# Attention scores of a two-layer encoder trunk: two stacked full-height products, or three half-height products per head

## The chip, the cores and the metric

The kernel runs on one core of one Trainium2 chip. The metric is the device time of one execution in microseconds; where several runs are given, their median. The profile is one execution recorded by the hardware profiler: TensorE's products and weight loads are listed apart (PE, PEld), VectorE is DVE, ScalarE is ACT, GpSimd is POOL, and SP is the queue that issues most transfers.

## What is computed

Two layers of an encoder trunk on 512 tokens of width 1024, in float32. In each layer a wide projection feeds three mixers in parallel, differential attention (4 heads, each with two query-key sets of 64 channels), a convolution module, and neighbourhood attention (8 heads of 64 channels on an 8 x 64 grid); gates merge them, and a gated feed-forward block and a gated input embedding follow. The parts that the change touches are the scores of the two attentions:

```python
# differential attention, per head: two score matrices from 64 channels each
s = jnp.einsum('bhcqd,bhckd->bhcqk', qi, k).astype(f32) * scale
a = jax.nn.softmax(s, axis=-1)
a = (a[:, :, 0] - lam * a[:, :, 1]).astype(v.dtype)
...
# neighbourhood attention, per head: 8 x 16 keys around each query, with a bias
s = jnp.einsum('bhwd,bhrwcd->bhwrc', q_r, kn).astype(jnp.float32) * scale
s = s + bias.transpose(0, 2, 1, 3)[None].astype(jnp.float32)
a = jax.nn.softmax(s.reshape(B, HC, GRID_W, KR * NA_KC), axis=-1)
```

## The kernel before

Everything is held transposed: channels on the 128 partitions, the 512 tokens along the free axis. A token's number in the kernel is its column times 8 plus its row, so that a neighbourhood is a window of keys: each of the four tiles of 128 queries sees 256 keys, which start at 0, 64, 192 and 256 (`KEY0`). TensorE multiplies in a reduced format (fp32r). To keep float32 accuracy every operand is split into a high part (rounded, on ScalarE) and a low part (the remainder, on VectorE); a product of two split operands takes three products, high x high, high x low and low x high (`mm3`, lines 177 to 179).

`layer` writes the order of TensorE's instructions by hand. Projections, gates and branches stream through `gemm`, and after every fourth chunk of three products a tick (12 products) passes. The attentions' units are generators which `later` puts into a queue; a unit starts a given number of ticks after its projection, with a gap to the next, and each `yield n` in it lets n ticks pass before it goes on. So the units' small products are dealt out between the projections' products of 512 columns. On the other engines a scheduler sets the order.

A pair of neighbourhood heads (`natten_in`) or one differential head (`diff_in`) has its queries and keys in one projection: 64 channels of one set (u = 0) on partitions 0 to 63 and of the other (u = 1) on 64 to 127. Before, the parts are written to tiles of their own ("kh" and "t", or "kh" and "rp"), and `stack` (line 660 issues the copies on SP's queue) builds stacked operands from them: for each set a query tile with the high part on 64 partitions and the low part on the other 64, a key tile in the same order, and a second key tile (`k2`, tag "x") in the opposite order. Then `scores` (line 811) needs two products over all 128 partitions for a set: the first gives high x high + low x low, the second high x low + low x high.

A neighbourhood unit (`natten_unit`) handles one head and one half of the queries, that is two query tiles: it loads one bias tile (line 702), makes the two score tiles, adds the bias and takes the maximum on VectorE (line 710), takes exponentials with their sums on ScalarE, then reciprocals (line 722) and scalings; two ticks later it transposes the probabilities on TensorE (lines 734 to 738), splits them, and two ticks later multiplies them with the values (lines 753, 754). A pair of heads has four units, a tick apart. A differential unit (`diff_unit`) handles one query tile of one head; `probs` makes its two score tiles of 512 keys, whose maxima VectorE takes (line 902). Score tiles lie in PSUM under the tag "sc", of which there are two, a bank each. SBUF tiles with a tag share as many buffers as the table `bufs` gives: qk 2, x 4, e 4, b 2, kh 2.

## Time and profile before

| | us |
|---|---|
| median of three runs (lowest, highest) | 1776.03 (1776.01, 1777.37) |
| span of the profiled execution | 1776.7 |
| HBM rate over the span | 125 GB/s |

The profiled execution's time is known as its span, from its first to its last instruction. A row of the page or of a view of the trace names the line, the engine, the operation, the tile written and the tiles read, the shape, the number of instructions, and their durations. Products overlap: a record goes on past the start of the next one, and the ends are modelled, so a product's cost in a stream is the distance between two starts. The rows themselves stand in the prediction, beside the sentences that use them.

### The profile page before, as it was taken

The numbers are of one execution on the slowest core, as the hardware profiler recorded it, in microseconds if no ns is written. First come the engines' busy times: TensorE is split into PE (matmuls) and PEld (weight loads), VectorE is DVE, ScalarE is ACT, GpSimd is POOL, SyncE is SP. The second block draws the span as 40 slices with busy tenths as digits, with TensorE's granted clock in tenths as the row PEclk, the third lists the DMA queues.
The fourth block names the chain that finished last, engine by engine and source line by source line (L and its number), as shares of the span: only waits on it lengthen the run. The fifth ranks groups of instructions, "written<-read, shape, count | busy, mean of one in ns | idle before, by whom it ended". The sixth has DMA issues, their size and how long they took to land.

```text
span 1776.7 us, 27451 instructions
## 1 busy us (share of the span) xinstructions
PE 1767.5 (99%) x10210; PEld 1559.6 (88%) x10210; DVE 1421.7 (80%) x2418; ACT 894.4 (50%) x1561; POOL 103.0 (6%) x146
## 2 busy tenths in 40 slices
PE   9999999999999999999999999999999999999998
PEld 7888888888899899998888888888888998989987
DVE  7878887998798587787776788889887976867776
ACT  5577555225565254454545765452356643534454
POOL 0000000000111010100000000000001110101000
PEclk9999999999999999999999999999999999999999
DMA  5666641334757366543447655423357664655332
GB/s 202 188 186 176 161 125 42 113 98 140 230 150 193 109 167 160 132 131 123 145 124 198 176 165 149 113 71 95 93 179 198 171 179 115 173 144 151 98 108 92
DMA packets 113509, 256.07 MB, mean 144 GB/s; under 512 B 14560, under 2 KB 19424, under 8 KB 113376
## 3 DMA queue, kind: packets, MB, share of 16 engines
q1 hardware_dynamic: 99984, 229.93, 42.3%
q0 software_dynamic: 12672, 23.07, 8.3%
q8 instruction: 81, 1.33, 0.3%
q10 hardware_dynamic: 720, 1.31, 0.2%
q14 instruction: 52, 0.43, 0.1%
HBM read 215.46 MB, written 7.34 MB: 125 GB/s over the span
## 4 chain that ended last, share of the span: by engine, by line
PE 96%; DVE 2%; ACT 1%; issue 0%; DMA 0%; POOL 0%; ACTq 0%; POOLq 0%; DVEq 0%
PE ffn_mm L1017 4%; PE ffn_mm L1019 4%; PE ffn_mm L177 4%; PE ffn_mm L179 4%; PE ffn_mm L178 4%; PE ffn_mm L1018 4%; PE ffn_sc L1019 3%; PE ffn_sc L1017 3%; PE ffn_sc L1018 3%; PE mergea_mm L177 2%; PE mergea_mm L178 2%; PE mergea_mm L179 2%; PE diff_sc L811 2%; PE gatec_mm L177 2%; PE gatec_mm L178 2%; PE gatec_mm L179 2%
## 5 line engine op out<-in xcount | busy, mean ns | idle before, releaser
L160 DVE SCALAR_TENSOR_TENSOR conv_z<-glu_z,pre_par,conv_z 128x512 f32<-128x512 f32 x240 | 179.4, 748 | 3.3
L143 ACT ACTIVATE ffn_wh<-ffn_wr 128x1024 fp32r<-128x1024 f32 (+1 forms) x92 | 92.7, 1014 | 111.7 <-PE ffn_mm L178 77.1
L987 POOL DMA_DIRECT2D ffn_qk<-w_fu x88 | 78.0, 990 | 605.7 <-DMA ffn_qk<-w_fu 414.7
L157 DVE TENSOR_TENSOR ffn_wl<-ffn_wr,ffn_wh 128x1024 fp32r<-128x1024 f32 (+1 forms) x92 | 107.4, 1173 | 5.4 <-ACT ffn_wh L143 4.9
L157 DVE TENSOR_TENSOR ffn_t<-ffn_mm,wo_rb 128x512 f32<-128x512 f32 (+1 forms) x64 | 38.6, 604 | 67.9 <-PE ffn_mm L179 67.8
L143 ACT ACTIVATE mergea_wh<-mergea_wr 128x1024 fp32r<-128x1024 f32 (+1 forms) x32 | 27.1, 846 | 96.8 <-PE mergea_mm L178 79.6
L143 ACT ACTIVATE ffn_wh<-ffn_qk 128x1024 fp32r<-128x1024 f32 x44 | 46.7, 1060 | 35.9 <-PE ffn_mm L178 15.7
L157 DVE TENSOR_TENSOR ffn_wl<-ffn_qk,ffn_wh 128x1024 fp32r<-128x1024 f32 x44 | 53.8, 1224 | 11.3 <-ACT ffn_wh L143 11.3
L157 DVE TENSOR_TENSOR ffn_t<-ffn_t,ffn_t 128x512 f32<-128x512 f32 (+1 forms) x46 | 31.3, 680 | 31.4 <-ACT ffn_t L143 30.9
L143 ACT ACTIVATE diff_a<-diff_sc,diff_s 128x512 f32<-128x512 f32 x32 | 22.0, 686 | 61.0 <-DVE diff_s L902 61.0
L177 PE MATMUL ffn_mm<-ffn_v,ffn_wh 128*128 128x512 f32 x132 | 51.4, 389 | 0.0
L178 PE MATMUL ffn_mm<-ffn_v,ffn_wh 128*128 128x512 f32 x132 | 51.4, 389 | 0.0
L179 PE MATMUL ffn_mm<-ffn_v,ffn_wl 128*128 128x512 f32 x132 | 51.3, 389 | 0.0
L177 PE MATMUL ffn_mm<-ffn_y,ffn_wh 128*128 128x512 f32 x132 | 51.3, 389 | 0.0
L178 PE MATMUL ffn_mm<-ffn_y,ffn_wh 128*128 128x512 f32 x132 | 51.3, 389 | 0.0
L179 PE MATMUL ffn_mm<-ffn_y,ffn_wl 128*128 128x512 f32 x132 | 51.3, 389 | 0.0
L1019 PE MATMUL ffn_mm<-wo_h,ffn_wl 128*128 128x256 f32 x176 | 49.8, 283 | 0.0
L1019 PE MATMUL ffn_sc<-wo_h,ffn_wl 128*128 128x256 f32 x176 | 49.8, 283 | 0.0
L1018 PE MATMUL ffn_mm<-wo_h,ffn_wh 128*128 128x256 f32 x176 | 49.8, 283 | 0.0
L1018 PE MATMUL ffn_sc<-wo_h,ffn_wh 128*128 128x256 f32 x176 | 49.8, 283 | 0.0
L1017 PE MATMUL ffn_sc<-wo_h,ffn_wh 128*128 128x256 f32 x176 | 49.8, 283 | 0.0
L1017 PE MATMUL ffn_mm<-wo_h,ffn_wh 128*128 128x256 f32 x176 | 49.8, 283 | 0.0
(876 smaller groups left out, 6588.6 us busy)
## 6 DMA issues: line engine op xcount, KB each, us to landing
ffn_qk<-w_fu POOLq DMA_DIRECT2D x88, 256.0 KB, 5.7
ffn_wr<-w_fg SPq DMA_DIRECT2D x44, 512.0 KB, 3.7
ffn_wr<-w_fd SPq DMA_DIRECT2D x32, 448.0 KB, 3.9
ffn_r<-w_fu SPq DMA_DIRECT2D x44, 256.0 KB, 3.7
ffn_qk<-w_fg SPq DMA_DIRECT2D x44, 256.0 KB, 4.3
ffn_qk<-w_fu SPq DMA_DIRECT2D x44, 256.0 KB, 4.6
natten_wr<-w_in SPq DMA_DIRECT2D x16, 512.0 KB, 4.3
natten_b<-bias SPq DMA_DIRECT2D x32, 256.0 KB, 4.0
```

The lines of the kernel that those rows point to most:

```text
L143: i = self.nc.scalar.activation(out, in_, func, **kw)
L157: return self.nc.vector.tensor_tensor(out, a, b, op)
L160: return self.nc.vector.scalar_tensor_tensor(out, a, s, b, op0, op1)
L177: mm(out, wh, ah, start=first, stop=False)
L178: mm(out, wh, al, start=False, stop=False)
L179: mm(out, wl, ah, start=False, stop=last)
L811: self.nc.tensor.matmul(out, st4[:, u, qs], st[:, ks], start=n == 0, stop=n == 1)
L987: nc.gpsimd.dma_start(q, wu[:, lo], accum_op=ALU.add)
L1017: mm(out, wh[:, c], bh, start=first and k == 0, stop=False, skip_group_check=True)
L1018: mm(out, wh[:, c], bl, start=False, stop=False, skip_group_check=True)
L1019: mm(out, wl[:, c], bh, start=False, stop=k == 3, skip_group_check=True)
```

## The change

- `natten_in` and `diff_in` write the high and the low parts straight into the query-key tile `st4`: index 0 and 1 are the queries' high and low parts, 2 and 3 the keys'. `stack` goes, with its copies and with `k2`. (`scores` stays in the file, but nothing calls it.)
- `both_scores` makes the scores of two sets at once: three products for each set (high x high, high x low, low x high), each over the 64 partitions on which its set lies, and in turn one of the lower half, one of the upper half. The two sets write to two score tiles.
- A neighbourhood unit handles both heads of a pair and one half of the queries: both heads' scores of the first query tile, a tick later those of the second; then reciprocals and scalings of both; two ticks later the first head's transposes and values (`natten_values`), and a tick later the second head's. There are two units for a pair, with a gap of two ticks.
- The bias lies sorted by pair and query tile, so that one transfer brings both heads. The probabilities of the second half of the queries lie in tiles of the tag "x" instead of "e".
- `probs` takes both score tiles first, makes their products together, and then goes on as before.

```diff
@@ -633,32 +633,21 @@
 
         self.phase = "natten"
         st4 = self.sb("qk", [P, 4, 512], F32R)
-        k2 = self.sb("x", [P, 2, 512], F32R)
         for s, off in enumerate((OFF_QC, OFF_KC)):
             ps = self.proj(off + pr * P)
             f = 1.0 if s else 0.125
-            nat, low = self.sb("kh", [P, 512], F32R), self.sb("t", [P, 512], F32R)
+            nat, low = st4[:, 2 * s], st4[:, 2 * s + 1]
             if pr == 0:
 
-                t = low.bitcast(F32)
+                t = self.sb("t", [P, 512])
                 self.stt(t, ps, f, self.rb, ALU.mult, ALU.mult)
                 ps, f = t, 1.0
             self.act(nat, ps, AF.Copy, scale=f)
             self.background(self.stt(low, ps, f, nat.bitcast(F32), ALU.mult, ALU.subtract),
                             self.bg["natten"])
-            self.stack(nat, low, st4[:, 2 * s:2 * s + 2], k2 if s else None)
         ys.append(self.sb("y", [P, 2, 512], F32R))
-        for n in range(4):
-            self.later(self.natten_unit(pr, n // 2, n % 2, st4, k2, st, ys[pr]), 6 if pr == 3 else 5 if pr else 10, 1)
-
-    def stack(self, nat, low, one, two):
-
-        for n, part in enumerate((nat, low)):
-            for st, r in ((one, 64 * n), (two, 64 - 64 * n)):
-                for u in range(2):
-                    if st is not None:
-                        self.nc.sync.dma_start(st[r:r + 64, u].bitcast(F32),
-                                               part[64 * u:64 * u + 64].bitcast(F32))
+        for half in range(2):
+            self.later(self.natten_unit(pr, half, st4, st, ys[pr]), 6 if pr == 3 else 5 if pr else 10, 2)
 
     def natten_v(self, st):
 
@@ -692,37 +681,49 @@
                     self.nc.sync.dma_start(vd[o:o + 64, n].bitcast(F32), edge.bitcast(F32))
             st["v", g] = vs[g], vd
 
-    def natten_unit(self, pr, half, u, st4, k2, st, y):
+    def natten_unit(self, pr, half, st4, st, y):
 
         nc, i = self.nc, self.i
-        mm = nc.tensor.matmul
-        head = 2 * pr + u
-        b = self.sb("b", [P, 2, NW])
-        with self.tc.high_priority(offset=100):
-            nc.sync.dma_start(b, self.a["bias"][i, head, half])
-        es = []
-        m = self.sb("s", [P, 6])
+        es, ms = ([], []), [self.sb("s", [P, 6]) for _ in range(2)]
         for t in range(2):
             qt = 2 * half + t
-            sc = self.ps("sc", (P, NW))
-            self.scores(sc, st4, k2, u, slice(qt * P, (qt + 1) * P),
-                        slice(KEY0[qt], KEY0[qt] + NW))
-            nc.vector.tensor_tensor_reduce(
-                out=b[:, t], in0=sc, in1=b[:, t], scale=-1.0, scalar=3.0e38,
-                op0=ALU.add, op1=ALU.min, accum_out=m[:, t:t + 1])
+            b = self.sb("b", [P, 2, NW])
+            with self.tc.high_priority(offset=100):
+                nc.sync.dma_start(b, self.a["bias"][i, pr, qt])
+            scs = [self.ps("sc", (P, NW)) for _ in range(2)]
+            self.both_scores(scs, st4, slice(qt * P, (qt + 1) * P),
+                             slice(KEY0[qt], KEY0[qt] + NW))
             wide = half != t
-            e = self.sb("e", [P, NW + 64 * wide])
-            own = slice(64 * (qt == 1), 64 * (qt == 1) + NW)
-            if wide:
-                pad = slice(0, 64) if qt == 1 else slice(NW, NW + 64)
-                nc.gpsimd.memset(e[:, pad], 0.0)
-            self.act(e[:, own], b[:, t], AF.Exp, table="exp", scale=-1.0, bias=m[:, t:t + 1],
-                     accum_out=m[:, 2 + t:3 + t])
-            es.append((e, e[:, own]))
-        nc.vector.reciprocal(m[:, 4:6], m[:, 2:4])
-        for t, (_, own) in enumerate(es):
-            self.act(own, own, AF.Copy, scale=m[:, 4 + t:5 + t])
+            if half:
+                both = self.sb("x", [P, 2, 512])
+            for u, (sc, m) in enumerate(zip(scs, ms)):
+                nc.vector.tensor_tensor_reduce(
+                    out=b[:, u], in0=sc, in1=b[:, u], scale=-1.0, scalar=3.0e38,
+                    op0=ALU.add, op1=ALU.min, accum_out=m[:, t:t + 1])
+                e = (both[:, u] if half else self.sb("e", [P, 512]))[:, :NW + 64 * wide]
+                own = slice(64 * (qt == 1), 64 * (qt == 1) + NW)
+                if wide:
+                    pad = slice(0, 64) if qt == 1 else slice(NW, NW + 64)
+                    nc.gpsimd.memset(e[:, pad], 0.0)
+                self.act(e[:, own], b[:, u], AF.Exp, table="exp", scale=-1.0, bias=m[:, t:t + 1],
+                         accum_out=m[:, 2 + t:3 + t])
+                es[u].append((e, e[:, own]))
+            if t == 0:
+                yield 1
+        for u, m in enumerate(ms):
+            nc.vector.reciprocal(m[:, 4:6], m[:, 2:4])
+            for t, (_, own) in enumerate(es[u]):
+                self.act(own, own, AF.Copy, scale=m[:, 4 + t:5 + t])
         yield 2
+        for u in range(2):
+            self.run(self.natten_values(pr, half, u, es[u], st, y))
+            if u == 0:
+                yield 1
+
+    def natten_values(self, pr, half, u, es, st, y):
+
+        nc = self.nc
+        mm = nc.tensor.matmul
         pt = self.ps("tr", (P, 2, 256))
         pt2 = self.ps("tr", (P, P))
         p2 = self.sb("a", [P, P], F32R)
@@ -810,6 +811,13 @@
         for n, st in enumerate((st4[:, 2 + u], k2[:, u])):
             self.nc.tensor.matmul(out, st4[:, u, qs], st[:, ks], start=n == 0, stop=n == 1)
 
+    def both_scores(self, outs, st4, qs, ks):
+
+        for n, (a, b) in enumerate(((0, 2), (0, 3), (1, 2))):
+            for u, out in enumerate(outs):
+                r = slice(64 * u, 64 * u + 64)
+                self.nc.tensor.matmul(out, st4[r, a, qs], st4[r, b, ks], start=n == 0, stop=n == 2)
+
     def diff_in(self, head, st, ys):
         self.phase = "diff"
         if head == 0:
@@ -819,7 +827,6 @@
                 self.nc.sync.dma_start(c, self.a["rope"][t])
                 st["tabs"].append(c)
         st4 = self.sb("qk", [P, 4, 512], F32R)
-        k2 = self.sb("x", [P, 2, 512], F32R)
         for s, off in enumerate((OFF_QA, OFF_KA)):
             ps = self.proj(off + head * P)
             raw, rot = self.sb("rp", [P, 512]), self.sb("rp", [P, 512])
@@ -830,22 +837,20 @@
             self.background(self.tt(raw, raw, st["tabs"][0], ALU.mult), self.bg["diff"])
             self.tt(rot, rot, st["tabs"][1], ALU.mult)
             self.tt(raw, raw, rot, ALU.add)
-            nat, low = self.sb("kh", [P, 512], F32R), raw.bitcast(F32R)
-            self.split(nat, low, raw)
-            self.stack(nat, low, st4[:, 2 * s:2 * s + 2], k2 if s else None)
+            self.split(st4[:, 2 * s], st4[:, 2 * s + 1], raw)
         box = dict(s0=self.sb("sm", [P, 4]))
         for qt in range(4):
-            self.later(self.diff_unit(head, qt, st4, k2, st, box, ys), 6 if head else 7, 2)
+            self.later(self.diff_unit(head, qt, st4, st, box, ys), 6 if head else 7, 2)
 
     def diff_v(self, g, st):
         self.phase = "diff"
         st["v", g] = self.values(self.a["w_va"][self.i, g], lambda v, a: ((v[:, 0:256], v[:, 256:512], a),))
 
-    def diff_unit(self, head, qt, st4, k2, st, box, ys):
+    def diff_unit(self, head, qt, st4, st, box, ys):
 
         nc, i = self.nc, self.i
         half, t = qt // 2, qt % 2
-        box[qt] = self.probs(st4, k2, qt, box["s0"])
+        box[qt] = self.probs(st4, qt, box["s0"])
         if t == 0:
             return
         yield 3
@@ -889,16 +894,16 @@
 
         yield from self.norm(sq, P, (1, 2), done, spread=False, eps=eps)
 
-    def probs(self, st4, k2, qt, s0):
+    def probs(self, st4, qt, s0):
 
 
         nc, i = self.nc, self.i
         qs = slice(qt * P, (qt + 1) * P)
         m = self.sb("s", [P, 10])
         es = []
-        for u in range(2):
-            sc = self.ps("sc")
-            self.scores(sc, st4, k2, u, qs, slice(0, 512))
+        scs = [self.ps("sc") for _ in range(2)]
+        self.both_scores(scs, st4, qs, slice(0, 512))
+        for u, sc in enumerate(scs):
             nc.vector.tensor_reduce(out=m[:, u:u + 1], in_=sc, op=ALU.max, axis=AX.X, negate=True)
             e = self.sb("e" if u else "a", [P, 512])
             self.act(e, sc, AF.Exp, table="exp", bias=m[:, u:u + 1],
@@ -1403,7 +1408,7 @@
         ok = (w[k][None, :] >= cs[q][:, None]) & (w[k][None, :] < cs[q][:, None] + NA_KC)
         out[:, :, qt] = np.where(ok, rpb[:, :, np.where(ok, ro, 0), np.where(ok, co, 0)],
                                  out[:, :, qt])
-    out = out.reshape(L, HC, 2, 2, P, NW).transpose(0, 1, 2, 4, 3, 5)
+    out = out.reshape(L, HC // 2, 2, 4, P, NW).transpose(0, 1, 3, 4, 2, 5)
     return np.ascontiguousarray(out)
 
 
```

## The prediction

> **What bounds the kernel now.** I read the head of the page first, then the waits of TensorE, then the two attention stages of layer 0.
>
> ```profile
> span 1776.7 us, 27451 instructions
> ...
> PE 1767.5 (99%) x10210; PEld 1559.6 (88%) x10210; DVE 1421.7 (80%) x2418; ACT 894.4 (50%) x1561; POOL 103.0 (6%) x146
> ...
> PEclk9999999999999999999999999999999999999999
> ...
> PE 96%; DVE 2%; ACT 1%; issue 0%; DMA 0%; POOL 0%; ACTq 0%; POOLq 0%; DVEq 0%
> ```
>
> TensorE is busy 1767.5 of 1776.7 us, at full clock, and the chain that ended last is 96% TensorE. A busy share of 99% alone could hide modelled ends, so the waits of that engine come next:
>
> ```profile
> PE pre_av L325 <- DVE pre_zeror L398: 1.1, 1, 1.1
> PE natten_tr L734 <- ACT natten_e L143: 0.3, 2, 0.2
> PE natten_tr L736 <- ACT natten_e L143: 0.3, 2, 0.2
> PE natten_tr L736 <- DVE natten_a L157: 0.2, 1, 0.2
> ```
>
> It waits 1.9 us in all, 1.1 of them at the start. The only waits of the attentions are 0.8 us, where the neighbourhood probabilities arrive late at their transposes. By stretches (both attentions' inputs and units; then the rest of differential attention and its neighbours):
>
> ```profile
> 70.00:172.00 102.00, 101.61 (x594) 88.73 (x593) 78.47 (x192) 74.20 (x179) 2.12 (x14) 1.00 0.69 188
> 172.00:320.00 148.00, 148.00 (x798) 127.07 (x798) 125.73 (x219) 76.93 (x154) 4.53 (x4) 1.00 0.41 113
> ```
>
> TensorE (the second number) fills both, ScalarE 74 of 102 us and VectorE 126 of 148. So the question is how much time the new score products take on TensorE and nothing else, unless another engine is made late.
>
> **The score products: what goes.** The line of scores has four rows of products, 128 of each width (64 of each row):
>
> ```profile
> L811 PE MATMUL natten_sc<-natten_qk x64: 277/283/366, 77.7 to 1043.5; 128*128 128x256 f32 x64
> L811 PE MATMUL natten_sc<-natten_x,natten_qk x64: 274/281/283, 77.8 to 1043.6; 128*128 128x256 f32 x64
> L811 PEld LDWEIGHTS diff_sc<-diff_qk x64: 187/188/192, 172.3 to 1167.3; 128*128 128x128 f32 x64
> L811 PE MATMUL diff_sc<-diff_qk x64: 389/396/478, 172.3 to 1167.5; 128*128 128x512 f32 x64
> L811 PE MATMUL diff_sc<-diff_x,diff_qk x64: 387/394/398, 172.6 to 1167.8; 128*128 128x512 f32 x64
> ```
>
> Their durations overlap, so a product's price is the distance to the next start, from the order of time:
>
> ```profile
> 77.68 0.28 PE L811 MATMUL natten_sc<-natten_qk 128*128 128x256 f32 x1
> 77.80 0.28 PE L811 MATMUL natten_sc<-natten_x,natten_qk 128*128 128x256 f32 x1
> 77.91 0.28 PE L811 MATMUL natten_sc<-natten_qk 128*128 128x256 f32 x1
> 78.03 0.28 PE L811 MATMUL natten_sc<-natten_x,natten_qk 128*128 128x256 f32 x1
> 78.15 0.40 PE L177 MATMUL natten_mm<-glu_h,natten_wh 128*128 128x512 f32 x1
> ...
> 172.63 0.39 PE L811 MATMUL diff_sc<-diff_x,diff_qk 128*128 128x512 f32 x1
> 172.86 0.39 PE L811 MATMUL diff_sc<-diff_qk 128*128 128x512 f32 x1
> 173.09 0.40 PE L811 MATMUL diff_sc<-diff_x,diff_qk 128*128 128x512 f32 x1
> 173.33 0.39 PE L177 MATMUL diff_mm<-glu_h,diff_wh 128*128 128x512 f32 x1
> ```
>
> Four neighbourhood products take 78.15 - 77.68 = 0.47 us, 0.117 each. A differential one takes (173.33 - 172.63) / 3 = 0.233, so four take 0.93. Each layer and attention has 16 such groups of four (four pairs of heads or four heads, four query tiles), so 32 groups of each: 32 x 0.47 = 15.0 us and 32 x 0.93 = 29.8 us, 44.8 us together.
>
> **What comes.** The same group becomes three pairs of products over 64 partitions, the two halves in turn. Before has no product of fewer than 128 rows, so a pair is bounded from both sides. If its two products run at the same time it costs one full product: 3 x 0.117 x 32 = 11.2 us and 3 x 0.233 x 32 = 22.4 us, 33.6 together, a gain of 11.2 us. If they run one after the other, six products per group cost twice that, 67.2 us, a loss of 22.4. I take the first: the two products read different partitions, hold different weights and write different banks (two tiles of "sc"), so neither needs what the other makes, and the list of waits shows no resource of TensorE at which products queue.
>
> The Trainium skill's page "TensorE: Matmul & The Clock Gate", "Part 3: Packing small matmuls — row/col tiling", says that products on different row groups run concurrently and gives 3.07x for four of them; no run here shows it. By it the pair would stand at the gain of 11.2 us.
>
> **The change of height.** Before and after each group are full-height products, so the array goes from full to half height and back: 2 x 64 = 128 times. The trace has no such change; the nearest one of kind is between transposes and products:
>
> ```profile
> 84.12 0.60 PE L736 MATMUL natten_tr<-pre_ident,natten_e 128*128 128x128 f32 x4
> 84.56 0.27 PE L738 MATMUL natten_tr<-pre_ident,natten_e 128*128 128x128 f32 x1
> 84.59 0.36 PE L811 MATMUL natten_sc<-natten_qk 128*128 128x256 f32 x1
> 84.79 0.28 PE L811 MATMUL natten_sc<-natten_x,natten_qk 128*128 128x256 f32 x1
> ```
>
> From the fifth transpose to the second score product are 0.23 us: a transpose, (84.56 - 84.12) / 4 = 0.11, and a score product, 0.12. That change costs nothing, and 0 is the lower end (a gain is excluded: nothing becomes shorter by a change). The upper end is that the array empties and the next weights are loaded only then: the tail of a record past the next start, 0.39 - 0.23 = 0.16 us, and one weight load, 0.19, so 0.35. I take the tail alone, 0.16: a transpose uses the array at the same height, so its 0 is the weaker neighbour, while weights are seen to load beside running products (loads busy 1559.6 us under 1767.5 us of products). 128 x 0.16 = 20.5 us (0 to 44.8).
>
> The page "TensorEngine Tiling (Array Packing)" of the Trainium skill, "Key Properties", speaks against the change: going over to another tiling mode, not just to another tile, drains the engine. It gives no price and no run here shows it; with the tail as the price the sum by that rule is the sum below, without it 1764.8 us.
>
> **The rest, costed at nothing.** The 192 copies that stacked queries and keys leave SP's queue (eight rows, 32 four times and 16 four times; the first and the last):
>
> ```profile
> L660 SPq DMA_DIRECT2D natten_qk<-natten_kh x32: 461/467/1325, 53.2 to 1011.7; - x32
> ...
> L660 SPq DMA_DIRECT2D diff_x<-diff_rp x16: 594/596/610, 163.3 to 1128.6; - x16
> ```
>
> No wait of TensorE names a DMA, and the units' starts are fixed by counted products, so the time that this frees (192 x about 0.55 us of issuing) goes into idle. The bias tiles stay 32 transfers of 256 KB, sorted by pair and query tile. The splits now write into the query-key tile itself, so ScalarE can wait for the scores of the head two before; those scores stand ahead of, or within 30 products (7 us) of, the end of the projection that the split follows, and in differential attention the rotation comes between. Behind such a wait stand the weight splits that TensorE needs, but the projections already run ahead; 0, at most 1 us for each of two heads a layer, 4 us.
>
> A neighbourhood unit of two heads goes as follows:
>
> ```profile
> L710 DVE CUSTOM_DVE_ANT_0 natten_b<-natten_sc,natten_b x64: 404/424/426, 78.1 to 1049.2; 128x256 f32<-128x256 f32 x64
> L143 ACT ACTIVATE natten_e<-natten_b,natten_s x64: 492/509/513, 79.1 to 1049.8; 128x256 f32<-128x256 f32 x64
> L143 ACT ACTIVATE natten_e<-natten_e,natten_s x64: 491/496/524, 80.7 to 1051.1; 128x256 f32<-128x256 f32 x64
> ```
>
> Before: two reductions, two exponentials, a reciprocal, two scalings, then transposes two ticks (24 products) later. After, the second half of a unit has the same two reductions and two exponentials, the first head's two scalings, and its transposes again two ticks later; the second head's scalings come behind and its transposes a tick later. The chain to the transposes keeps its length; 0, and where it is tight already (the four waits of 0.2 us) up to the two extra scalings, 4 x 1.0 = 4 us.
>
> **The sum.** 0 - 11.2 + 20.5 = +9.3 us. The profile's span of 1776.7 becomes 1786.0; it lies 0.7 above the median of 1776.0, inside the runs' 1776.0 to 1777.4, and I forecast 1786, not separating the two.
>
> **Rivals.** One, faster: the array changes its height for little. The place is the first product after each of the 128 changes; the price that decides is 11.2 / 128 = 0.088 us. At 0 it is 1764.8, at 0.06 (half a narrow product) 1772.5. For it: the transposes' 0, and weight loads that run beside products. Against: the narrow groups last only 0.35 us, so nothing in a group hides a price at both its ends.
>
> Two, much slower, the change not doing what it says: pairs don't overlap, because loads and products are issued in one line and each waits for the one before. 1776.0 + 22.4 = 1798.4 with free changes, 1818.9 with the tail, 1843 with the upper end. For it: no record of before has two products streaming at once, starts being 0.117 or 0.233 apart throughout. Against: all those products use all rows.
>
> Three, no change: the price lies at 0.06 to 0.115 us and eats the gain, 1772.5 to 1779.5.
>
> **How the numbers follow.** The forecast, overlap with a price of 0.115 to 0.35, has 0.37 and its own range 1779.5 to 1810; rival one 0.33; rival two 0.23; rival three 0.07. A difference under 0.2% (3.6 us) can't be told from none, which makes faster 0.33, within 0.07, slower 0.60. The range 1766 to 1812 leaves out the cheapest changes and the upper half of rival two, some 0.15.
>
> **What would show it.** In the order of time inside a group of six, starts in pairs with 0.23 us (wide) or 0.12 us (narrow) from pair to pair show the overlap; six starts that far apart show rival two. The distance from the sixth product to the projection behind it, and into the first, over 0.23 or 0.12, is the price of a change; if it is under 0.088 I am wrong about the sign. The line of scores should then take 54 us of TensorE's time where it took 44.8. If the groups agree and the time doesn't, the waits of TensorE on ScalarE (transposes of the neighbourhood) and on VectorE (score tiles not free) must have grown past the 1.9 us, and the terms put at nothing are where I went wrong.

## The result, and the profile after

The changed kernel takes 1799.95 us, the median of four runs (1799.67 to 1800.23); the kernel before takes 1776.70 beside it (1776.01 to 1778.10). The ratio is 1.0131 (95% interval 1.0116 to 1.0145): slower by 23.2 us where the forecast said 9.3. The profiled spans differ by 21.5 us.

The head of the page of the changed kernel:

```profile
span 1798.2 us, 27334 instructions
...
PE 1786.5 (99%) x10338; PEld 1550.0 (86%) x10338; DVE 1424.8 (79%) x2418; ACT 898.1 (50%) x1561; POOL 102.1 (6%) x146
...
PEclk9999999999999999999999999999999999999999
...
PE 93%; DVE 3%; ACT 3%; issue 1%; DMA 0%; POOL 0%; SPq 0%; ACTq 0%; POOLq 0%; DVEq 0%
```

The clock is full as before (0.999 in the mean of both), so nothing of this difference comes from it. TensorE is still busy 99%, but only 93% of the chain of waits is TensorE where it was 96%: VectorE, ScalarE and issue have 7% together. The waits of TensorE in the changed kernel (total us, times, longest):

```profile
PE natten_tr L735 <- DVE natten_pt L157: 2.7, 8, 0.4
PE natten_tr L737 <- DVE natten_a L157: 1.2, 2, 0.6
PE pre_av L325 <- DVE pre_zeror L398: 1.1, 1, 1.1
PE natten_sc L819 <- DVE natten_s L700: 1.0, 2, 0.5
```

They are 6.0 us where they were 1.9. The first two are transposes of the neighbourhood probabilities whose PSUM tiles VectorE has not yet split; the last is a score tile that VectorE has not yet reduced. The first of the two stretches:

```profile
70.00:172.00 102.00, 99.82 (x582) 81.64 (x581) 73.45 (x178) 68.79 (x164) 1.37 (x12) 1.00 0.42 122
```

TensorE (the second number) no longer fills it: 99.82 of 102 us against 101.61. VectorE (the fourth) is less busy there than before, 73.45 us against 78.47, so it is not its amount of work that makes TensorE wait. The line of scores, duration in ns as lowest/median/highest:

```profile
L819 PE MATMUL natten_sc<-natten_qk x192: 271/279/384, 77.6 to 1061.9; 64*128 64x256 f32 x192
L819 PE MATMUL diff_sc<-diff_qk x192: 385/394/501, 179.6 to 1190.5; 64*128 64x512 f32 x192
```

The products have the durations that they had over 128 partitions (279 and 394 ns). What differs is the distance of the starts. In the order of time, one narrow and one wide group of the changed kernel (start, us, and six products in one row):

```profile
77.25 0.39 PE L179 MATMUL natten_mm<-glu_h,natten_wl 128*128 128x512 f32 x1
77.57 0.62 PE L819 MATMUL natten_sc<-natten_qk 64*128 64x256 f32 x6
78.12 0.50 PE L177 MATMUL natten_mm<-glu_h,natten_wh 128*128 128x512 f32 x1
78.46 0.40 PE L178 MATMUL natten_mm<-glu_h,natten_wh 128*128 128x512 f32 x1
...
243.09 0.39 PE L179 MATMUL gatec_mm<-glu_h,gatec_wl 128*128 128x512 f32 x1
243.41 0.97 PE L819 MATMUL diff_sc<-diff_qk 64*128 64x512 f32 x6
244.31 0.50 PE L177 MATMUL gatec_mm<-glu_h,gatec_wh 128*128 128x512 f32 x1
244.64 0.40 PE L178 MATMUL gatec_mm<-glu_h,gatec_wh 128*128 128x512 f32 x1
```

The nine starts of two such groups, in ns from the product ahead, worked out from the single records:

```
                   ahead | pair 1  | pair 2  | pair 3  | next two
narrow (at 77.25)      0 | 318 322 | 542 547 | 658 663 |  868 1206
wide   (at 243.09)     0 | 318 321 | 653 663 | 888 898 | 1215 1552
```

Read it from the left. The two products of a pair start 3 to 10 ns apart: the halves do run at the same time. From the second pair to the third are 0.116 and 0.235 us, the distance of full products: a pair costs one. But the first start is 0.32 us after the product ahead, not 0.23; from the first pair to the second is 0.105 more than a pair; from the last pair to the next full product 0.09 more; and that product has a record of 0.50 instead of 0.39, and the one behind it starts 0.34 later instead of 0.23. So one change of height costs 0.09 + 0.11 = 0.20 us, and each group pays it twice. That the 0.09 is the array running empty is not shown by a row; the distance is. The weight loads of the same moment show what the 0.11 is:

```profile
77.03 0.19 PEld L179 LDWEIGHTS natten_mm<-glu_h,natten_wl 128*128 128x128 f32 x1
77.57 0.42 PEld L819 LDWEIGHTS natten_sc<-natten_qk 64*128 64x128 f32 x6 [0.35 <-issue]
78.12 0.19 PEld L177 LDWEIGHTS natten_mm<-glu_h,natten_wh 128*128 128x128 f32 x1
```

The weights of line 179 load at 77.03, beside the product ahead, and their own product starts 0.22 us later, at 77.25. The first weights of the group load at 77.57, where their own product's record begins, after 0.35 us of an idle loader; those of line 177 load at 78.12, where the record of theirs begins. At a change of height the load is not made ahead.

A group with its two changes is thus 78.46 - 77.25 = 1.21 us less two wide slots of 0.23, 0.75 (it was 0.47), and 244.64 - 243.09 = 1.55 less the same, 1.09 (it was 0.93). The medians over the 32 groups of each width are 0.752 and 1.098. The array's part of the loss is 64 x 2 x 0.20 = 25.6 less the 11.2 that overlap gains: 14.4 us.

### The profile page after: what moved, and what is told of

The parts are those of the page before. It is cut to its first block, busy times and chain, and to the rows that moved or that the text cites. A ratio compares the mean times of both kernels' runs of the same rounds, so it can differ in the third digit from the quotient of the medians.

```text
span 1798.2 us, 27334 instructions
## 1 busy us (share of the span) xinstructions
PE 1786.5 (99%) x10338; PEld 1550.0 (86%) x10338; DVE 1424.8 (79%) x2418; ACT 898.1 (50%) x1561; POOL 102.1 (6%) x146
## 4 chain that ended last, share of the span: by engine, by line
PE 93%; DVE 3%; ACT 3%; issue 1%; DMA 0%; POOL 0%; SPq 0%; ACTq 0%; POOLq 0%; DVEq 0%
PE ffn_mm L1022 4%; PE ffn_mm L1024 4%; PE ffn_mm L178 4%; PE ffn_mm L177 4%; PE ffn_mm L179 4%; PE ffn_mm L1023 4%; PE ffn_sc L1024 3%; PE ffn_sc L1022 3%; PE ffn_sc L1023 3%; PE mergea_mm L177 2%; PE mergea_mm L178 2%; PE mergea_mm L179 2%; PE gatec_mm L177 2%; PE diff_sc L819 2%; PE gateb_mm L177 2%; PE gatec_mm L178 2%
```

## The experiments

**Theories.** Mine: a change of height costs 0.20 us wherever it is made (14.4 us in all), the halves overlap because their products alternate; and the rest, 21.5 - 14.4 = 7.1 us of the span and nearly 9 of the medians, is TensorE waiting for engines whose order of work has changed. Rivals: the whole loss is the array's, a higher price per change; the change of height costs less by itself than in the group; the order of issue makes no difference to the overlap.

**The price of a change by itself.** The kernel before, with one product of 128 columns ahead of each of its 64 groups, overwritten by the group:

```diff
+        if touch:
+            r, few = slice(0, 64), slice(ks.start, ks.start + P)   # slice(0, 128) in the second kernel
+            self.nc.tensor.matmul(out[:, 0:P], st4[r, u, qs], st4[r, 2 + u, few], start=True, stop=True)
         for n, st in enumerate((st4[:, 2 + u], k2[:, u])):
```

> The kernel before, with one half-height product of 128 columns in front of each of the 64 groups of four full-height score products; its result is overwritten by the group's first product, so nothing else changes. Theory (each change of height costs 0.20 us, 0.09 for emptying the array and 0.11 for a weight load that nothing hides, whatever runs at half height): 64 x (2 x 0.20 + 0.06) = 29 us more than before. Rival A (the tail of 0.16 us that the prediction took): 64 x (0.32 + 0.06) = 24 us. Rival B (the exposed load belongs to pairs, a change costs 0.09): 64 x (0.18 + 0.06) = 15 us.

> The control of the former: the same added product over all 128 partitions. Every theory: 64 x 0.06 = 4 us more than before, up to 7 us if a product of 128 columns costs 0.11 like a transpose. If it costs much more, the added product delays something and the former run says little of a change of height.

With half height 1802.43 us, 25.3 more than the 1777.10 before beside it (ratio 1.0144, 1.0129 to 1.0159); with full height 1785.84, 8.7 more (1.0051, 1.0036 to 1.0066). In the order of time, first the half-height kernel, then the full one:

```profile
192.65 0.39 PE L179 MATMUL diff_mm<-glu_h,diff_wl 128*128 128x512 f32 x1
192.97 0.32 PE L812 MATMUL diff_sc<-diff_qk 64*128 64x128 f32 x1
193.22 0.50 PE L814 MATMUL diff_sc<-diff_qk 128*128 128x512 f32 x1
193.56 0.39 PE L814 MATMUL diff_sc<-diff_x,diff_qk 128*128 128x512 f32 x1
```

```profile
189.94 0.39 PE L179 MATMUL diff_mm<-glu_h,diff_wl 128*128 128x512 f32 x1
190.16 0.22 PE L812 MATMUL diff_sc<-diff_qk 128*128 128x128 f32 x1
190.22 0.45 PE L814 MATMUL diff_sc<-diff_qk 128*128 128x512 f32 x1
190.50 0.39 PE L814 MATMUL diff_sc<-diff_x,diff_qk 128*128 128x512 f32 x1
```

The time lies between the theory's 29 and a rival's 24, so the rows decide. The same 0.32, 0.50 and 0.34 as in the changed kernel stand around a single small product. It adds 193.56 - 192.65 - 2 x 0.23 = 0.45 us to its group: two changes at 0.20 and some 0.05 of its own. The full-height one adds 190.50 - 189.94 - 0.46 = 0.10, in the mean of all groups 0.12. So there is a price of the change itself, which needs neither the group of six nor the units: the distances over all groups grew by 28.3 us, as the theory had it, and the time by 25.3; the other 3 us have no row.

The size is less sure here than in the changed kernel. Over its control, whose distances grew by 7.7 us, the half height adds 20.6 us, 0.16 a change, and that is rival A's price. The rows give 0.20 because they count 0.06 for the added product (190.16 to 190.22) and not the 0.05 by which the product behind it takes longer in the control too (190.50 - 190.22 = 0.28 in place of 0.23); that the half-height kernel already contains this 0.05 in its exposed load is argued, not tried. One small product thus shows 0.16 to 0.20. The full-height kernel lies a little above its expectation: 7.7 us of products, and 2.2 us of new waits on VectorE where 0.8 went.

**Everything but the height.** The changed kernel with four full-height products in place of the six, on the same tiles:

```diff
-        for n, (a, b) in enumerate(((0, 2), (0, 3), (1, 2))):
-            for u, out in enumerate(outs):
-                r = slice(64 * u, 64 * u + 64)
-                self.nc.tensor.matmul(out, st4[r, a, qs], st4[r, b, ks], start=n == 0, stop=n == 2)
+        for u, out in enumerate(outs):
+            for n, (a, b) in enumerate(((0, 2), (0, 3))):
+                self.nc.tensor.matmul(out, st4[:, a, qs], st4[:, b, ks], start=n == 0, stop=n == 1)
```

> The changed kernel with its units, tiles, copies and order, but each group of six half-height products replaced by four full-height ones on the unstacked tiles (the scores then mix the two sets of channels and leave out one cross product; the work per group on TensorE is that of before). Theory (array 14.4 us, the remaining 8.6 us are waits that the two-head unit makes): 1776.7 + 8 = 1783 to 1786 us, with TensorE's waits at the neighbourhood's transposes as in the changed kernel. Rival (the waits come from the groups that last longer): 1776 to 1778 us, with the waits of before.

It took 1790.60 us, 13.5 more than before (1.0075, 1.0058 to 1.0092), above what either theory gave. So the steps that the prediction put at nothing cost 13.5 us when the array's price is taken out. Its waits of TensorE:

```profile
PE natten_tr L735 <- DVE natten_pt L157: 4.7, 8, 1.8
PE diff_sc L818 <- ACT diff_e L143: 1.8, 2, 0.9
PE natten_tr L737 <- DVE natten_a L157: 1.2, 2, 0.6
...
```

With two smaller rows that is 9.6 us, 3.6 more than in the changed kernel, and 1.7 us more go to a short stretch of half clock (the last part of this section). These 5.3 us are why the two costs, 13.5 and 14.4, don't add to 27.9 but to 23.2. A likely reason is that the engines behind TensorE catch up while it is held up at its changes of height; waits and array price are not separate terms.

**Each attention by itself.** The change in differential attention alone (on the kernel before), in neighbourhood attention alone, and in differential attention alone with full-height products as above. The core of the first:

```diff
-        k2 = self.sb("x", [P, 2, 512], F32R)
...
-            nat, low = self.sb("kh", [P, 512], F32R), raw.bitcast(F32R)
-            self.split(nat, low, raw)
-            self.stack(nat, low, st4[:, 2 * s:2 * s + 2], k2 if s else None)
+            self.split(st4[:, 2 * s], st4[:, 2 * s + 1], raw)
...
+        scs = [self.ps("sc") for _ in range(2)]
+        self.both_scores(scs, st4, qs, slice(0, 512))
```

> Differential attention alone by half-height products, the neighbourhood as before. Theory: 32 groups of 1.10 us where 0.93 stood, 5.4 us more than before, and no new waits, since its units are unchanged: about 1782 us. Rival (the waits come with unstacked tiles or with groups that last longer, in either attention): 5.4 + about 4 = 9 to 10 us more.

> The neighbourhood alone by half-height products, with its units of two heads; differential attention as before. Theory: 32 groups of 0.75 where 0.48 to 0.50 stood, 8 us, and the waits at the neighbourhood's transposes, 4 to 6 us: 1789 to 1791. Rival (all waits come from differential attention's unstacked tiles): 1785.

> Differential attention without stacked tiles, as in the former run of it alone, but with four full-height products per group as before (the scores then mix the two sets and leave out one cross product); the neighbourhood as before. Theory now (the waits beyond the array come from another order on VectorE and ScalarE once the splits write straight into the query-key tile, not from half height): 13.4 - 5.5 = about 8 us more than before, with the waits of the neighbourhood's score products on VectorE. Rival (they come from longer groups): 0 to 2 us more.

Differential attention alone took 1790.48 us (+13.4; 1.0078, 1.0063 to 1.0093), more than either theory gave, with full height 1784.97 (+8.0; 1.0046, 1.0031 to 1.0061): the height is worth 5.5 us, the 32 x (1.10 - 0.925) = 5.6 of the array. Both have the same long waits. Neighbourhood attention alone took 1798.35 (+21.4; 1.0123, 1.0108 to 1.0138), far above the 1789 to 1791 expected: to the array's 32 x (0.752 - 0.49) = 8.4 (0.49 is the mean group of before) come 6.2 us of waits for VectorE's splits of the smaller transposed tile ("a"), 3.1 for those of the larger one ("pt"), and 3.4 us of half clock. The parts lose 34.8 us and the whole 23.2, so what a part costs depends on the order around it: the listed waits of the parts grew by 13.6 us and those of the whole by 4.1, and half clock costs the parts 5.1 us and the whole none.

The 8.0 us can be followed. With full-height products in differential attention alone, TensorE has one new wait that stands out:

```profile
PE natten_sc L811 <- DVE natten_s L710: 4.9, 4, 2.1
```

The neighbourhood's score tile is reduced late. VectorE around that place, in the kernel before:

```profile
152.53 0.42 DVE L710 CUSTOM_DVE_ANT_0 natten_b<-natten_sc,natten_b 128x256 f32<-128x256 f32 x1 [0.73 <-PE natten_sc L811]
...
155.48 0.69 DVE L157 TENSOR_TENSOR diff_rp<-diff_rp,diff_r 128x512 f32<-128x512 f32 x1
```

and in the kernel with the stacking gone:

```profile
152.15 0.68 DVE L157 TENSOR_TENSOR diff_rp<-diff_rp,diff_r 128x512 f32<-128x512 f32 x1
...
156.90 0.42 DVE L710 CUSTOM_DVE_ANT_0 natten_b<-natten_sc,natten_b 128x256 f32<-128x256 f32 x1
```

Before, the reductions stand ahead of the rotation of the next head; now the rotation goes first and the reduction comes 4 us later. SP's queue shows what moved, before (the first two rows) and with the stacking gone (the last):

```profile
149.50 1.14 SPq L660 DMA_DIRECT2D diff_qk<-diff_kh  x2
...
151.98 1.24 SPq L829 DMA_DIRECT2D diff_rp<-diff_rp  x2
```

```profile
147.56 1.78 SPq L835 DMA_DIRECT2D diff_rp<-diff_rp  x3
```

The copies of line 660 held the last two of the rotation's four transfers back until 151.98; without them the last three are issued in a row from 147.56, and the rotation is ready before the reductions. That the one is the cause of the other is argued from these rows; that the order is the cause of the wait was tried.

**The order of VectorE set back.** The fourth pair's score reductions of the neighbourhood go ahead in the order that the scheduler makes for VectorE, and nothing else is changed, with full and with half height in differential attention:

```diff
-            nc.vector.tensor_tensor_reduce(
+            with self.tc.high_priority(offset=150 if pr == 3 else 0):
+                nc.vector.tensor_tensor_reduce(
```

> Differential attention unstacked at full height (scores mixed, one cross product left out), with only the score reductions of the fourth pair of neighbourhood heads put ahead on VectorE. Theory (TensorE waits there for score tiles because VectorE takes the rotations first): the wait of 4.9 us goes, 1785.0 - 5 = 1778 to 1781. Rival (another wait of the same size takes its place, since VectorE or ScalarE lacks the time in this stretch): 1784 to 1787.

> Differential attention by half-height products with the same two places moved. Theory: 5.5 us above the run beside it, 1783 to 1787. Rival: 1789 to 1792.

They took 1779.71 us (ratio 1.0015, 1.0005 to 1.0024) and 1784.60 (1.0043, 1.0027 to 1.0060), both as the theory had it. VectorE of the full-height one:

```profile
153.68 0.42 DVE L711 CUSTOM_DVE_ANT_0 natten_b<-natten_sc,natten_b 128x256 f32<-128x256 f32 x1
...
155.04 0.68 DVE L157 TENSOR_TENSOR diff_rp<-diff_rp,diff_r 128x512 f32<-128x512 f32 x1
```

The reductions stand ahead of the second rotation again, and the wait of 4.9 us has no row any more. 5.3 of the 8.0 us were that order: the listed waits fell from 7.7 to 4.1 us, and 1.7 us of half clock behind the long wait went with it. The 4.9 us between the two kernels are the array's price of the 32 wide groups (5.5 by the rows).

**The same for the whole change.** Three tries to free the waits of the changed kernel: reductions and splits ahead on both engines (with half and with full height), and the two heads' values two ticks apart in place of one:

```diff
+                with self.tc.high_priority(offset=100):
+                    nc.vector.tensor_tensor_reduce(
...
+        with self.tc.high_priority(offset=100):
+            self.split(pp[:, 0], pp[:, 1], pt)
+            self.split(p2[er], p2[eo], pt2[er])
...
             if u == 0:
-                yield 1
+                yield 2   # the third kernel, without the rest
```

> The changed kernel, with the neighbourhood's score reductions and the splits of its transposed probabilities put ahead of other work in the order that the scheduler makes for VectorE and ScalarE; TensorE's order and all work are unchanged. Theory (8.6 us of the loss are waits of TensorE behind VectorE's order, the array's price is 14.4): the waits at the neighbourhood's transposes and scores fall from 4.9 us to under 1 us, and the time to 1792 to 1795. Rival (the waits are the units' own chain, whatever the order): 1798 to 1801.

> The same order of reductions and splits in the changed kernel with four full-height products per group (the scores then mix the two sets and leave out one cross product). Theory: without half height and without the waits nothing is left, 1777 to 1780. Rival (the units of two heads cost time by themselves): 1787 or more, as without the order. Against the run with half height, the difference is the price of the array, 14 us by theory.

> The changed kernel, with two ticks in place of one between the first head's transposes and values and the second's, so that the transposes' banks have twice the time to come free. Theory (the waits at the second transposes are for banks that VectorE empties late): those waits vanish, 1794 to 1797. Rival (the waits move to the next step behind): 1799 to 1802.

None came out as the theory had it: 1802.80 us (1.0146), 1784.76 (1.0045) and 1828.67 (1.0291). Waits of TensorE in the first, and then in the third:

```profile
PE diff_sc L820 <- ACT diff_e L143: 5.4, 2, 3.0
PE natten_mm L755 <- DVE natten_y L157: 2.1, 2, 1.0
```

```profile
PE natten_tr L735 <- DVE natten_pt L157: 19.5, 8, 4.1
```

In the first the waits of the transposes are gone and others stand in their place: differential attention's score tiles now wait for ScalarE's exponentials, and the values' tiles for VectorE. Its distance to the second is 18.0 us, not the array's 14: the first has 5.1 us of half clock and the second none. In the third, more room between the two heads made the wait on the splits seven times as long. As a control the same order was given to the kernel before, and to the two kernels with the change in differential attention:

> The kernel before with the same order on VectorE and ScalarE, nothing else. Theory: it has 0.8 us of such waits to lose, 1775 to 1777.5. Rival (the order itself makes new waits): 1779 or more, and then the two runs beside it can't be read as an order repaired.

> The kernel with differential attention unstacked at full height (scores mixed as there, one cross product left out), and the neighbourhood's score reductions and splits put ahead on VectorE and ScalarE. Theory (its 8 us are TensorE's waits for score tiles, because VectorE takes the rotations first): back to the kernel before, 1776 to 1779, the wait of 4.9 us gone. Rival (the units can't go faster without the stacking copies between them): 1783 to 1786.

> Differential attention alone by half-height products, with the same order on VectorE and ScalarE. Theory: only the array's price of 32 groups remains, 32 x (1.10 - 0.92) = 5.5 us above the former run without half height: 1782 to 1784. Rival as there: 1788 to 1791.

They took 1785.54 us (1.0052, 1.0034 to 1.0070), 1787.69 and 1793.95. Of the first:

```profile
PE natten_tr L737 <- ACT natten_e L143: 6.7, 6, 1.2
```

A kernel with not one instruction added or removed on TensorE loses 8.8 us to another order on VectorE and ScalarE. The transposes wait for scalings: around 161 us a weight split of 1.04 us now stands on ScalarE between a unit's two scalings (161.25, 161.67, 162.61), which before follow each other (162.37). The other two have the same row with 6.6 and 6.7 us, so they don't tell what their own waits cost. Last, only VectorE's half of the splits and the fourth pair's reductions, a short distance ahead (60) and a longer one (150):

> The changed kernel; VectorE's part of the splits of the transposed probabilities, and the score reductions of the fourth pair, put ahead by a short distance. Theory (8.6 us of the 23 are waits behind VectorE's order): the waits at transposes and scores fall below 1.5 us and the time to 1793 to 1797. Rival (they move elsewhere): 1799 or more.

> The same, put ahead by a longer distance. Theory and rival as beside it; if the two differ by more than 2 us, the order matters but isn't governed by this distance alone.

1800.90 us (1.0134, 1.0115 to 1.0152) and 1798.54 (1.0120, 1.0101 to 1.0138), a miss again: the transposes still wait 2.3 and 2.5 us, and the values wait 3.4 and 2.4 us for their tiles. Which order would free the whole change's waits stays open.

What the transposes wait for can be read one step further back. In the changed kernel, ScalarE, VectorE and TensorE around one of these waits:

```profile
145.15 1.70 ACT L143 ACTIVATE natten_x<-natten_x,natten_s 128x256 f32<-128x256 f32 x4
146.76 0.58 ACT L143 ACTIVATE natten_pt<-natten_tr 128x512 fp32r<-128x512 f32 x1
...
147.37 0.69 DVE L157 TENSOR_TENSOR natten_pt<-natten_tr,natten_pt 128x512 fp32r<-128x512 f32 x1 [1.92 <-ACT natten_pt L143]
...
148.11 0.33 PE L735 MATMUL natten_tr<-pre_ident,natten_x 128*128 128x128 f32 x1 [0.43 <-DVE natten_pt L157]
```

VectorE's split, for which TensorE waits, isn't late by VectorE's order: VectorE sat idle for 1.92 us until ScalarE's half of the same split was done. ScalarE took it 1.84 us after the transposes that it reads, behind the four scalings of the next unit, two for each head. So it is in 7 of the 8 waits of line 735 (2.5 of 2.7 us; in four of them a weight split stands between the scalings), in all eight of the full-height variant, and in all eight of the last two kernels, which moved VectorE's half alone and kept the waits; the kernel that moved both halves lost them. The other row, 1.2 us at line 737, is VectorE's order: the split of the smaller tile stands behind a rotation (152.48), and with VectorE's half put ahead that row is gone. The theory of the order trials, that the waits are all VectorE's order, was wrong for the larger part. No kernel moved the scalings alone.

**Alternation, and the price of a pair.** The changed kernel with three products of the lower half and then three of the upper, and with each group issued twice:

```diff
-        for n, (a, b) in enumerate(((0, 2), (0, 3), (1, 2))):
-            for u, out in enumerate(outs):
-                r = slice(64 * u, 64 * u + 64)
+        for u, out in enumerate(outs):
+            r = slice(64 * u, 64 * u + 64)
+            for n, (a, b) in enumerate(((0, 2), (0, 3), (1, 2))):
```

```diff
-        for n, (a, b) in enumerate(((0, 2), (0, 3), (1, 2))):
+        for n, (a, b) in enumerate(((0, 2), (0, 3), (1, 2)) * 2):
...
-                self.nc.tensor.matmul(out, st4[r, a, qs], st4[r, b, ks], start=n == 0, stop=n == 2)
+                self.nc.tensor.matmul(out, st4[r, a, qs], st4[r, b, ks], start=n % 3 == 0, stop=n % 3 == 2)
```

> The changed kernel with the same six half-height products per group, but the three of the lower half first and then the three of the upper half. Theory (neighbouring products of different halves run at the same time, of the same half one after the other): only the third and the fourth overlap, five slots in place of three: 32 x 2 x 0.231 + 32 x 2 x 0.117 = 22 us more than the changed kernel, less what shorter waits give back, 1815 to 1822. Rival (the order doesn't matter, the array works on both halves anyhow): 1800. If half-height products never overlapped, this would also be 1800.

> The changed kernel with each group of six issued twice in a row; the second set overwrites the first, so the result stays. Theory (a pair of half-height products costs one full product, 0.231 or 0.117, once the first is under way; the 0.4 us belong to the change of height): 64 groups gain three pairs, 32 x 3 x (0.231 + 0.117) = 33 us more than the changed kernel, less what shorter waits give back, so 1828 to 1833. Rival (a pair has a price above a full product, 0.05 each, because the second load isn't hidden): 33 + 64 x 3 x 0.05 = 43 us more, 1840 or more.

The halves apart took 1807.94 us (1805.42 to 1809.06; 1.0173, 1.0158 to 1.0188), 8 more than the changed kernel and not the 22 of six products in a row. The starts of one wide group (ns), and the row of another:

```
ahead | pair 1  | pair 2  | pair 3  | next two
    0 | 319 329 | 654 663 | 889 899 | 1215 1549
```

```profile
179.29 0.97 PE L819 MATMUL diff_sc<-diff_qk 64*128 64x512 f32 x6
```

The starts are in pairs as before, 9 or 10 ns apart, and the row of six lasts 0.97 us as before: on the array the order of issue makes no difference, and my theory fell. Most of the 8 us stand elsewhere: the largest new wait of TensorE is that of differential attention's scores for ScalarE's exponentials, 3.5 us (all listed waits grew by 2.1), and 5.1 us are half clock behind those waits (the last part of this section).

The groups issued twice took 1837.67 us (1.0341, 1.0324 to 1.0358), 37.7 more. One narrow and one wide group:

```profile
178.60 0.98 PE L819 MATMUL natten_sc<-natten_qk 64*128 64x256 f32 x12
179.50 0.50 PE L177 MATMUL diff_mm<-glu_h,diff_wh 128*128 128x512 f32 x1
...
187.68 1.66 PE L819 MATMUL diff_sc<-diff_qk 64*128 64x512 f32 x12
189.27 0.50 PE L177 MATMUL diff_mm<-glu_h,diff_wh 128*128 128x512 f32 x1
```

From the first of them to the next product are 0.90 us where it was 78.12 - 77.57 = 0.55, and 1.59 where it was 0.90. By the median group, three more pairs cost 1.788 - 1.098 = 0.69 us (wide) and 1.107 - 0.752 = 0.355 (narrow): 0.230 and 0.118 a pair, 33.4 us over all groups. A pair has no price but that of one full product. What is left of a group is its two changes: (1.098 - 0.69) / 2 and (0.752 - 0.355) / 2, 0.20 us each. The time lies between the theory's 1833 and the rival's 1840; the listed waits (7.4 us of them behind the neighbourhood's splits) grew by 3.7 us and half clock costs 5.1, more than the 4.3 us that the pairs leave.

**The clock behind long waits.** The changed kernel has the full clock up to its last few microseconds, but several of the kernels tried here don't. In differential attention alone at full height, the second layer's wait of 2.1 us for a score tile ends at 1040.05. The clock (the number behind the busy times) before, in and behind the stretch that follows:

```profile
1036.50:1040.50 4.00, 1.88 (x14) 1.53 (x13) 3.88 (x9) 1.05 (x3) 0.00 (x0) 1.00 0.48 131
1040.60:1043.90 3.30, 2.90 (x13) 2.91 (x14) 1.29 (x8) 2.58 (x9) 0.00 (x0) 0.50 0.31 79
1044.00:1047.30 3.30, 3.30 (x27) 3.16 (x27) 1.23 (x6) 2.31 (x5) 0.15 (x1) 1.00 0.25 79
```

At half clock products of 256 columns start 0.21 us apart (1041.59, 1041.80), behind it 0.12 (1044.20, 1044.32). The stretch lasts 3.4 us and so costs about half of that, 1.7. All such stretches in these traces (apart from one at the end of every kernel) last 3.4 or 6.8 us and begin 1.7 to 5.4 us after the start of a wait of 1.7 us or more, or of two close together of 1.2 and 1.0; but waits of up to 2.8 us also passed without one, and what decides is not shown. With them the profiled spans add up as follows (us over the kernel before; array by the medians, waits by their rows; the last column has no row):

| kernel | span | array | waits | half clock | left |
|---|---|---|---|---|---|
| changed kernel | 21.5 | 14.4 | 4.1 | 0 | 3.0 |
| changed kernel at full height | 12.5 | 0 | 7.7 | 1.7 | 3.1 |
| differential attention alone | 11.7 | 5.5 | 5.1 | 1.7 | -0.6 |
| differential attention alone at full height | 6.0 | 0 | 5.8 | 1.7 | -1.5 |
| neighbourhood alone | 19.8 | 8.4 | 8.5 | 3.4 | -0.5 |
| halves apart | 30.3 | 14.4 | 6.2 | 5.1 | 4.6 |
| groups issued twice | 59.8 | 47.8 | 7.8 | 5.1 | -0.9 |

A long wait thus can cost more than its own row says; the waits of the changed kernel, 0.6 us at most behind its start, carry no such stretch.

## Why the prediction was half right

- **Pairs overlap: right.** They start 3 to 10 ns apart and cost 0.230 and 0.118 each, so the gain of 11.2 us is there. Rival two (no overlap) is refuted by the same rows. The Trainium skill's page "TensorE: Matmul & The Clock Gate", "Part 3: Packing small matmuls — row/col tiling", has concurrent tiles at some 4 ns from start to start; this trace agrees, with 3 to 10.
- **The change of height: right in kind and sign, too small.** The term was 0.16 us (the tail of a record), 20.5 in all; it measured 0.20, 25.6 in all. The step that failed is the choice to take the tail alone because weights are seen to load beside running products. At a change they don't: 0.09 of a late start and 0.11 of a load that nothing hides. The prediction's upper end had that mechanism, at 0.35; the sizes of both its parts were too large. The rule of the Trainium skill's page "TensorEngine Tiling (Array Packing)", "Key Properties", that a change of mode drains the engine, fits the 0.09; the page has no price and says nothing of the load at a change. Rival one (under 0.088) and rival three (to 0.115) fall.
- **The line of scores** was to take 54 us where it took 44.8; by the medians it takes 32 x 1.10 + 32 x 0.752 = 59.3, with both changes of height in it.
- **"The rest, costed at nothing": wrong.** 23.2 - 14.4 = 8.8 us. The prediction named this as the place where it would fail, with the waits of TensorE past 1.9 us, and there it failed. Two of its steps are at fault. It said that the time freed on SP's queue "goes into idle", since no wait of TensorE names a DMA: but with the copies gone the rotations overtook the score reductions on VectorE, and in differential attention alone that order cost 5.3 us, shown by setting it back. And it said that the chain of a two-head unit to its transposes keeps its length, and looked for its risk at ScalarE's scalings. The scalings are the right place, but their own transposes don't wait for them any more. What waits is a step further on: the four scalings of a two-head unit stand on ScalarE in front of the split of the head before, whose PSUM tile the next transposes need (2.5 of the 2.7 us at line 735). That is read from the trace and borne out by the two ways of moving the splits; no kernel moved the scalings alone, and every order that was tried put another wait in the place of this one. The 1.2 us at line 737 are the rotations on VectorE again.
- **What the 8.8 us consist of.** The listed waits grew by 4.1 us. The distances over all groups, with the waits inside them, grew by 16.5 us, 2.1 above the array's price, of which 1.0 is the listed wait of the scores. So some 18 to 20 of the 21.5 us between the spans have a place; the rest has no row.

## What to carry to other kernels

Half-height products on both halves are worth it only where many follow one another: here a wide group saves 0.93 - 0.69 = 0.24 us and its two changes of height cost 0.40, so two wide groups side by side would about break even (that was worked out, not tried; it takes four score banks where there are two). In a kernel whose TensorE is fed just in time, a step that removes work from a queue isn't free because that queue was idle anyway: ask what becomes ready earlier, and whom it overtakes on the engine behind. A mere change of order cost this kernel 8.8 us, so where parts are tried by themselves, each needs a control that has the same structure without the disputed cost. The row of a wait names the engine that came last; whether that engine was itself idle, and for whom, decides which engine's order to change. And before the times of two trials are subtracted, look at the clock in each.

## What the hardware showed that was not expected

The two halves of the array run as two streams: with three products of one half issued ahead of three of the other, their starts still fall together in pairs, 9 or 10 ns apart, and the group takes the same 0.97 us. A full-height product behind a half-height one, or the reverse, starts 0.09 us late and has its weight load in the open for 0.11 us, with six half-height products between two changes or with twelve; with a single one of 128 columns the price is 0.16 to 0.20 us a change. And a wait of TensorE of some 2 us can be followed by 3.4 us at a granted clock of 0.50, which cost 1.7 us more.
